# HGRN2's products inside a token tile, cut to 32 keys by their own 32 queries, in four column groups of TensorE

## The chip, the cores and the metric

The kernel runs on one core of one Trainium2 chip. The metric is the device time of one execution in microseconds (us). All times of the profile are counted from the start of the profiled span.

## What is computed

One layer of a decoder: an HGRN2 group of heads (a gated linear recurrence) and an NSA group (sparse attention) side by side, an output projection, and a gated MLP. 512 tokens, 1024 channels. The change touches the HGRN2 group only: 4 heads of width 128, where every key channel of a head has its own decay at each token.

```python
def step(S, inp):                      # per chunk of 64 tokens
    qi, ki, vi, bi = inp               # bi: running sum of the log decays
    o_inter = einsum('bhtk,bhkv->bhtv', qi * exp(bi), S)
    diff = bi[:, :, :, None, :] - bi[:, :, None, :, :]
    dec = where(causal, exp(minimum(diff, 0.0)), 0.0)
    A = einsum('bhtsk,bhsk->bhts', dec * qi[:, :, :, None, :], ki)
    o = o_inter + einsum('bhts,bhsv->bhtv', A, vi)
    ...
```

A holds, for each query token t and each earlier key token s, the product of q and k under the decay between them. The decay depends on the channel, so A is no plain product of two matrices.

## The kernel before

The kernel works on four token tiles of 128 tokens. For HGRN2 it builds, per head and tile, the full 128 × 128 matrix A (tile `hgA`, keys on the partitions, queries in the columns) by halving: first the diagonal (a token with itself), then for L = 1, 2, 4, ..., 64 the products of the keys in an even block of L tokens with the queries in the odd block next to it. At each level the keys carry their decay up to the boundary between the two blocks and the queries theirs from that boundary on, so at each level one plain product serves all blocks of a tile. After each level, keys and queries are multiplied by the decay of a whole block (`tot`), which prepares the next level.

`hg_levels(pr, res)` does this for a pair of heads (`pr` 0 or 1). The second head of a pair (j = 1) has its tokens within a tile in reverse order, so that the blocks that give keys in one head and those of the other interleave, and `early_keys` packs the keys of both heads into one tile `hgE` of full width. One matmul per token tile then makes the products of 128 keys (64 of each head) with 128 queries (64 of each), of which only the blocks next to each other are wanted; a predicated copy on VectorE (L1138, by a mask of constants) picks these out of PSUM (tile `lev`) and puts them into `hgA`. So a level is:

- four matmuls on TensorE (L1129, a block of rows "lev<-hgQ,hgE"), 128 × 128 each, in float32;
- on VectorE (DVE): the keys times their decay (L1130, L1133), the predicated copy (L1138), the queries times theirs (L1141), the next block decay (L1147);
- on ScalarE (ACT): the keys of the next level (L1098, `hgE`).

The diagonal takes four matmuls for each head of the pair (L1109) and a multiplication by the identity for each (L1111).

What surrounds it: the attention of NSA (scores `S`, transposes `F`, values `oT`, at L969 to L1055), the input projections (`pT`, at L141 to L143) and the compression branch (`cps`, L884) run interleaved with the levels. The order is written out by hand: each of these is a Python generator, and a string `ORDER` of letters says which one takes its next step; "l" is `hg_levels(0)` and "m" is `hg_levels(1)`. Each engine then works through its instructions in exactly that order, with semaphores between engines. `G` takes a tile from a ring of 32 buffers of SBUF, `PS` one from the eight PSUM banks.

Some products of the kernel already use part of the columns of TensorE, with the output in the matching partitions of PSUM, so that several such products stand side by side: `values` (L1055, 64 stationary columns, the two heads of a couple in partitions 0 to 63 and 64 to 127), `cmp_hidden` (L884, 64 columns) and `ada_row` (L1293, 32 columns, four groups).

After the levels, `hgA` is the stationary operand of the output products `hgo` (L1224), together with the state between the tiles (L1227).

Of the kernel before, what the change touches and what calls it, by code (L numbers as in the profile page):

```python
# [13 lines left out]
U8 = mybir.dt.uint8  # L14
AF = mybir.ActivationFunctionType
ALU = mybir.AluOpType
# [3 lines left out]
P = 128  # L20
T = 512
NT = T // P
# [37 lines left out]
LEVELS = (1, 2, 4, 8, 16, 32, 64)  # L60
# [3 lines left out]
C_LMASK = 136  # L64
C_CMASK = C_LMASK + sum(P // n for n in LEVELS)
# [10 lines left out]
def shape_constants():  # L76
    c = np.zeros((P, C_COLS), np.float32)
    p = np.arange(P)
    c[:, C_IDENT:C_IDENT + P] = np.eye(P, dtype=np.float32)
    m = [np.broadcast_to(((t[:, None] // (2 * L) == np.arange(64 // L)[None])  # L80
                          & ((t[:, None] // L) % 2 == 0))[:, None], (P, NT, 64 // L)).reshape(P, -1)
         for L in LEVELS for t in (p, P - 1 - p)]
    c[:, C_LMASK:C_CMASK] = np.ascontiguousarray(np.concatenate(m, axis=1).astype(np.uint8)).view(np.float32)
    n = np.arange(32)
# [12 lines left out]
def hybrid_layer_kernel(ctx: ExitStack, tc: tile.TileContext, d: dict, out: bass.AP, dbg=None):  # L97
# [21 lines left out]
    def PS(s="ps"):  # L119
        return psum.tile([P, 512], F32, tag="b", name=nm(s))  # L120
# [142 lines left out]
    mask = cb[:, C_LMASK:C_CMASK].bitcast(U8)  # L263
# [837 lines left out]

    def hg_levels(pr, res):
        TT, KS, QP = HG[pr]
        AD = G([2, NT, P], s="hgA")
        for j in range(2):
            ps = PS("lev")
            for i in range(NT):
                sl = slice(i * P, (i + 1) * P)
                pe.matmul(ps[:, sl], KS[:, j, sl], QP[:, j, sl], start=True, stop=True)  # L1109
            yield  # L1110
            ve.tensor_tensor(AD[:, j], ps.rearrange("p (i t) -> p i t", i=NT),  # L1111
                             ident[:, ::1 - 2 * j].unsqueeze(1).to_broadcast([P, NT, P]), ALU.mult)
# [7 lines left out]
        while L < P:  # L1120
# [3 lines left out]
            m0 = sum(512 // n for n in LEVELS if n < L)  # L1124
            ps = PS("lev")
            pv = ps.rearrange("p (j i n l) -> p j i n l", j=2, i=NT, l=L)
            qt = QP.rearrange("p j (i n two l) -> p j i n two l", i=NT, two=2, l=L)
            for i in range(NT):
                pe.matmul(pv[:, :, i], E[:, i * P:(i + 1) * P], qt[:, :, i, :, 1], start=True, stop=True)  # L1129
# [5 lines left out]
            if 2 * L < P and EPOS == 0:  # L1135
                E = early_keys(KS, 2 * L)
            yield
            ve.copy_predicated(AD.rearrange("p j i (n two l) -> p (j i n) two l", two=2, l=L)[:, :, 1],  # L1138
                               mask[:, m0:m0 + 512 // L].unsqueeze(2).to_broadcast([P, 512 // L, L]),
                               ps.rearrange("p (n l) -> p n l", l=L))  # L1140
# [540 lines left out]
```

## Time and profile before

| | |
|---|---|
| device time, median of 3 runs | 702.78 us (702.70 to 703.16) |
| span of the profiled execution | 701.6 us (the runs' times include about 1.2 us around it) |
| granted TensorE clock | 1.000 |
| busy: PE / PEld / DVE / ACT / POOL | 99% / 82% / 66% / 46% / 16% of the span |
| level products, L1129 | 112 records from 140.8 to 253.0 us |
| diagonal products, L1109 | 32 records from 124.9 to 173.8 us |
| predicated copies, L1138 | 14, 893 ns on average, 12.5 us |

PE is the matmul side of TensorE and PEld its weight loads, POOL is GpSimd, SP issues DMAs. Matmul records overlap in the profile, so a duration of one record is longer than what it adds; what one adds is read from the distance between starts, or from the pieces of the chain of work that ended last. The note "x8" behind a name is the count of records.

### The profile page before, as it was taken

How to read it: one execution, taken by the hardware profiler on the slowest of the kernel's cores; microseconds unless marked ns; L12 is line 12 of the kernel's file. 1: busy time of each engine (PE TensorE's matmuls, PEld its weight loads, DVE VectorE, ACT ScalarE, POOL GpSimd, SP SyncE). 2: the span in 40 equal slices, each digit the busy share in tenths (PEclk: the TensorE clock that was granted, in tenths of full speed). 3: DMA queues.
4: the chain of work that ended last, by engine and by line, in shares of the span. 5: the costliest groups of instructions: out<-in, count | busy, mean ns of one | idle time of the engine just before them, and what ended most of it. 6: DMA issues, size and time to landing. Idle time of an engine off the chain costs nothing.

```text
span 701.6 us, 10075 instructions
## 1 busy us (share of the span) xinstructions
PE 692.7 (99%) x3863; PEld 576.1 (82%) x3864; DVE 461.0 (66%) x882; ACT 324.8 (46%) x618; POOL 108.8 (16%) x101
## 2 busy tenths in 40 slices
PE   8999999999999999999999999999999999999997
PEld 4668898788888889888988888888888888888886
DVE  5588989987889879688756556665555554224224
ACT  5554446565676778345543353444443443111210
POOL 2005021200000000100037527611010110000000
PEclk9999999999999999999999999999999999999999
DMA  9996452558212125243053545424424233134301
GB/s 286 293 290 195 123 160 88 193 192 270 76 47 93 62 77 204 79 143 82 21 166 106 150 126 145 143 69 120 113 67 121 77 103 121 60 94 177 119 32 60
DMA packets 100485, 90.18 MB, mean 129 GB/s; under 512 B 5788, under 2 KB 83412, under 8 KB 100438
## 3 DMA queue, kind: packets, MB, share of 16 engines
q1 hardware_dynamic: 100181, 89.44, 41.6%
q8 instruction: 30, 0.49, 0.3%
q14 instruction: 18, 0.14, 0.1%
q10 hardware_dynamic: 256, 0.11, 0.1%
HBM read 87.43 MB, written 2.11 MB: 128 GB/s over the span
## 4 chain that ended last, share of the span: by engine, by line
PE 81%; DVE 11%; DMA 3%; SPq 2%; ACT 1%; issue 1%; POOL 0%; ACTq 0%; DVEq 0%; POOLq 0%
PE u L142 11%; PE u L143 11%; PE u L141 11%; PE dn L143 6%; PE dn L142 6%; PE dn L141 6%; PE oT L1055 3%; PE F L1027 3%; PE pT L141 2%; PE pT L143 2%; PE pT L142 2%; PE lev L1129 2%; PE oh L141 2%; PE oh L143 2%; PE oh L142 2%; PE S L969 1%
## 5 line engine op out<-in xcount | busy, mean ns | idle before, releaser
L138 DVE TENSOR_TENSOR wlo<-raw,whi 128x1024 fp32r<-128x1024 f32 (+1 forms) x87 | 111.4, 1280 | 130.4 <-ACT whi L137 129.9
L141 PE MATMUL u<-h2h,whi 128*128 128x512 f32 (+1 forms) x360 | 136.7, 380 | 0.0
L142 PE MATMUL u<-h2l,whi 128*128 128x512 f32 (+1 forms) x360 | 136.7, 380 | 0.0
L143 PE MATMUL u<-h2h,wlo 128*128 128x512 f32 (+1 forms) x360 | 136.7, 380 | 0.0
L137 ACT CAST whi<-raw 128x1024 fp32r<-128x1024 f32 (+1 forms) x87 | 89.8, 1032 | 99.6 <-PE dn L143 80.1
L141 PEld LDWEIGHTS u<-h2h,whi 128*128 128x128 f32 x360 | 67.7, 188 | 12.9
L143 PEld LDWEIGHTS u<-h2h,wlo 128*128 128x128 f32 x360 | 67.7, 188 | 12.7
L142 PEld LDWEIGHTS u<-h2l,whi 128*128 128x128 f32 x360 | 67.7, 188 | 12.7
L142 PE MATMUL dn<-wlo,gT 128*128 128x512 f32 (+1 forms) x160 | 62.1, 388 | 0.0
L143 PE MATMUL dn<-whi,gT 128*128 128x512 f32 (+1 forms) x160 | 62.1, 388 | 0.0
L141 PE MATMUL dn<-whi,gT 128*128 128x512 f32 (+1 forms) x160 | 62.0, 388 | 0.0
L1568 POOL TENSOR_TENSOR y<-y,y 128x512 f32<-128x512 f32 x22 | 28.4, 1290 | 165.7 <-DVE y L1563 165.7
L353 POOL TENSOR_TENSOR hrs<-hrs,mhalf 128x4 f32<-128x4 f32 (+2 forms) x16 | 18.3, 1153 | 203.5 <-DVE hrs L352 203.5
L137 ACT CAST gT<-y 128x512 fp32r<-128x512 f32 x20 | 12.4, 621 | 71.7 <-POOL y L1568 71.7
L138 DVE TENSOR_TENSOR gT<-y,gT 128x512 fp32r<-128x512 f32 x20 | 15.0, 750 | 43.0 <-ACT gT L137 43.0
L141 PE MATMUL pT<-hT,whi 128*128 128x512 f32 x96 | 39.2, 408 | 0.0
L143 PE MATMUL pT<-hT,wlo 128*128 128x512 f32 x96 | 37.6, 392 | 0.0
L142 PE MATMUL pT<-hT,whi 128*128 128x512 f32 x96 | 37.5, 391 | 0.0
L1566 ACT ACTIVATE y<-y 128x512 f32<-128x512 f32 x22 | 13.9, 632 | 49.7 <-DVE y L1563 49.7
L142 PEld LDWEIGHTS dn<-wlo,gT 128*128 128x128 f32 x160 | 30.0, 188 | 6.5 <-DVE wlo L138 0.2
L141 PEld LDWEIGHTS dn<-whi,gT 128*128 128x128 f32 x160 | 30.0, 188 | 6.2
L143 PEld LDWEIGHTS dn<-whi,gT 128*128 128x128 f32 x160 | 30.0, 188 | 6.1
(371 smaller groups left out, 1443.6 us busy)
## 6 DMA issues: line engine op xcount, KB each, us to landing
raw<-in_w_up SPq DMA_DIRECT2D x44, 512.0 KB, 4.1
aw<-in_w_ada SPq DMA_DIRECT2D x24, 512.0 KB, 3.9
raw<-in_w_down SPq DMA_DIRECT2D x10, 1024.0 KB, 5.0
ada<-in_w_ada SPq DMA_DIRECT2D x32, 256.0 KB, 6.0
raw<-in_w_in SPq DMA_DIRECT2D x7, 1024.0 KB, 6.2
x<-in_x SPq DMA_DIRECT2D x8, 512.0 KB, 4.6
raw<-in_w_cmp SPq DMA_DIRECT2D x8, 512.0 KB, 4.6
raw<-in_w_out SPq DMA_DIRECT2D x4, 1024.0 KB, 5.9
```

Source lines behind the costliest of these rows:

```text
L137: sc.copy(hi, src)
L138: (eng or ve).tensor_tensor(lo, src, f32(hi), ALU.subtract)
L141: pe.matmul(o, ah, bh, start=start, stop=False, skip_group_check=True)
L142: pe.matmul(o, ah, bl, start=False, stop=False, skip_group_check=True)
L143: pe.matmul(o, al, bh, start=False, stop=stop, skip_group_check=True)
L353: gp.tensor_tensor(o, o, mhalf[:, 0:n], ALU.pow)
L969: pe.matmul(o, QS[i][:, h], KK[g, 0][:, 0:i + 1, bsl], start=True, stop=False)
L1027: pe.transpose(ps[:, j * P:(j + 1) * P], src[:, j * P:(j + 1) * P], ident)
L1055: pe.matmul(oTs[i][r:r + 64, h // 2], VV[:, j, b, g], src[:, q * P:(q + 1) * P], start=(h == 0 and b == 0 and j == 0), stop=False, skip_gr ...
L1129: pe.matmul(pv[:, :, i], E[:, i * P:(i + 1) * P], qt[:, :, i, :, 1], start=True, stop=True)
L1566: sc.activation(y, y, AF.Silu)
L1568: gp.tensor_tensor(ys[0], ys[0], y, ALU.mult)
```

## The change

The 128 × 128 matrix A of a tile is seen as 4 × 4 blocks of 32 tokens. The diagonal and levels 1 to 16 only concern the four blocks on its diagonal: 32 keys with their own 32 tokens. `small_products` makes just these: 16 matmuls a level (four tiles, four groups g) with 32 stationary columns, partitions 32g to 32g + 31 of PSUM as output, and 32 moving columns (16 queries of each head), or, for the diagonal, 32 matmuls of 32 × 32 at one time for both heads. The results gather in one block of 32 columns of `hgA` (`own`, columns 32 to 63 of each tile), by a multiplication with a small diagonal mask and by predicated copies of 128 elements in place of 512. After level 16, `spread` on GpSimd copies the blocks from there to their places and clears the rest; a clear of all of `hgA` (GpSimd too) stands at the start. Levels 32 and 64 (`large_products`) make 16 matmuls of 32 × 32 and 8 of 64 × 64; their results are all wanted, and `large_out` copies them by turns with ScalarE and VectorE. The masks of the constants shrink, and `ORDER` stays as it is.

```diff
-LEVELS = (1, 2, 4, 8, 16, 32, 64)
+LEVELS = (1, 2, 4, 8, 16)
...
+    def columns(ap, off, *dims):
+        return bass.AP(ap.tensor, ap.offset + off, [tuple(ap.ap[0]), *dims])
+
+    def small_products(ps, K, QP, L):
+        for i in range(NT):
+            for g in range(4):
+                o, k = ps[32 * g:32 * g + 32], slice(i * P + 32 * g, i * P + 32 * g + 32)
+                if L:
+                    pe.matmul(columns(o, 16 * i, (64, 2), (L, 16 // L), (1, L)), K[:, k],
+                              columns(QP, i * P + 32 * g + L, (T + 32 * (3 - 2 * g), 2), (2 * L, 16 // L), (1, L)),
+                              start=True, stop=True, skip_group_check=True)
+                else:
+                    for j in range(2):
+                        q = i * P + 32 * (3 - g if j else g)
+                        pe.matmul(o[:, j * P + 32 * i:j * P + 32 * i + 32], K[:, j, k], QP[:, j, q:q + 32], start=True,
+                                  stop=True, skip_group_check=True)
+
+    def large_products(ps, E, QP, L):
+        for i in range(NT):
+            for g in range(P // L):
+                j, n = g % 2, g // 2
+                if j:
+                    n = 64 // L - 1 - n
+                q = i * P + 2 * L * n + L
+                pe.matmul(ps[L * g:L * g + L, i * L:i * L + L], E[:, i * P + L * g:i * P + L * g + L],
+                          QP[:, j, q:q + L], start=True, stop=True, skip_group_check=True)
+
+    def large_out(ps, AD, L):
+        for g in range(P // L):
+            j, n = g % 2, g // 2
+            if j:
+                n = 64 // L - 1 - n
+            (ve.tensor_copy if g % 2 else sc.copy)(AD[L * g:L * g + L, j, :, 2 * L * n + L:2 * L * n + 2 * L],
+                                                   ps[L * g:L * g + L, 0:NT * L].rearrange("p (i t) -> p i t", i=NT))
+
+    def spread(AD):
+        for j in range(2):
+            for g in range(4):
+                w = 3 - g if j else g
+                if w != 1:
+                    gp.tensor_copy(AD[32 * g:32 * g + 32, j, :, 32 * w:32 * w + 32],
+                                   AD[32 * g:32 * g + 32, j, :, 32:64])
+            gp.memset(AD[64 - 64 * j:P - 64 * j, j, :, 32:64], 0.0)
+
     def hg_levels(pr, res):
         TT, KS, QP = HG[pr]
         AD = G([2, NT, P], s="hgA")
-        for j in range(2):
-            ps = PS("lev")
-            for i in range(NT):
-                sl = slice(i * P, (i + 1) * P)
-                pe.matmul(ps[:, sl], KS[:, j, sl], QP[:, j, sl], start=True, stop=True)
-            yield
-            ve.tensor_tensor(AD[:, j], ps.rearrange("p (i t) -> p i t", i=NT),
-                             ident[:, ::1 - 2 * j].unsqueeze(1).to_broadcast([P, NT, P]), ALU.mult)
+        gp.memset(AD, 0.0)
+        own = AD[:, :, :, 32:64]
+        ps = PS("lev")
+        small_products(ps, KS, QP, 0)
+        yield
+        ve.tensor_tensor(own, ps[:, 0:256].rearrange("p (j i t) -> p j i t", j=2, i=NT),
+                         diag32.unsqueeze(2).to_broadcast([P, 2, NT, 32]), ALU.mult)
+        yield
         ve.tensor_tensor(QP, QP, TT, ALU.mult)
...
-            for i in range(NT):
-                pe.matmul(pv[:, :, i], E[:, i * P:(i + 1) * P], qt[:, :, i, :, 1], start=True, stop=True)
+            (small_products if L < 32 else large_products)(ps, E, QP, L)
...
-            ve.copy_predicated(AD.rearrange("p j i (n two l) -> p (j i n) two l", two=2, l=L)[:, :, 1],
-                               mask[:, m0:m0 + 512 // L].unsqueeze(2).to_broadcast([P, 512 // L, L]),
-                               ps.rearrange("p (n l) -> p n l", l=L))
+            if L < 32:
+                m0 = sum(P // n for n in LEVELS if n < L)
+                ve.copy_predicated(own.rearrange("p j i (n two l) -> p (j i) n two l", two=2, l=L)[:, :, :, 1],
+                                   mask[:, m0:m0 + P // L].rearrange("p (a n) -> p a n", a=2 * NT).unsqueeze(3)
+                                   .to_broadcast([P, 2 * NT, 16 // L, L]),
+                                   ps[:, 0:P].rearrange("p (a n l) -> p a n l", a=2 * NT, l=L))
+            else:
+                large_out(ps, AD, L)
+            if L == 16:
+                spread(AD)
```

How this moves instructions, at three places. First TensorE at the diagonal of the first pair (a name is output<-moving operand, stationary operand; a shape is that of the output, and "x3" counts further equal calls). Before:

```order
L1109 MATMUL lev_1488<-hgQ_1237,hgK_730 128x128 [waits DVE_49,Activation_49]
L1109 MATMUL lev_1488<-hgQ_1237,hgK_730 128x128 x3
L834 MATMUL ps_1493<-cb,dst_1372 128x128 [waits DVE_49,Activation_49]
...
L863 MATMUL ps_1528<-cb,wpe_698 128x32 [waits DMAHW5_49,DVE_49,Activation_49]
L1109 MATMUL lev_1545<-hgQ_1237,hgK_730 128x128 [waits Activation_49]
L1109 MATMUL lev_1545<-hgQ_1237,hgK_730 128x128 x3
L141 MATMUL pT_1550<-hT_289,whi_1444 128x512 [waits PE_49,Activation_49]
```

And with the change, at the same place:

```order
L1122 MATMUL lev_1489<-hgQ_1237,hgK_730 32x32 [waits DVE_49,Activation_49]
L1122 MATMUL lev_1489<-hgQ_1237,hgK_730 32x32 x31
L838 MATMUL ps_1522<-cb,dst_1372 128x128 [waits DVE_49,Activation_49]
...
L867 MATMUL ps_1557<-cb,wpe_698 128x32 [waits DMAHW5_49,DVE_49,Activation_49]
L144 MATMUL pT_1574<-hT_289,whi_1444 128x512 [waits Activation_49]
```

The second head's diagonal moves up to the first's place, and its own place is empty. Next, VectorE and ScalarE at level 32 of the first pair; before, VectorE:

```order
L1138 COPY_PREDICATED hgA_1487<-cb,lev_2484 128x16x32
L1141 TENSOR_TENSOR hgQ_1237<-hgQ_1237,hgtot_2392 128x16x32
L1010 RECIPROCAL su_2478<-su_2478 128x2 [waits Activation_49]
L1011 TENSOR_TENSOR su_2478<-su_2478,gates 128x2 [waits DVE_49]
L974 ISA pt_2585,mx_2584<-S_2581,cmask 128x384 [waits PE_49]
```

With the change, VectorE:

```order
L1141 COPY hgA_1487<-lev_2622 32x4x32 [waits Activation_49]
L1141 COPY hgA_1487<-lev_2622 32x4x32 [waits Activation_49,Pool_49]
L1196 TENSOR_TENSOR hgQ_1237<-hgQ_1237,hgtot_2518 128x16x32
L1014 RECIPROCAL su_2616<-su_2616 128x2
L1015 TENSOR_TENSOR su_2616<-su_2616,gates 128x2 [waits DVE_49]
```

and ScalarE, where before only the two `hgE` copies stood:

```order
L1102 COPY hgE_2705<-hgK_1435 128x2x32x8 [waits DVE_49]
L1141 COPY hgA_1487<-lev_2622 32x4x32 [waits Pool_49]
L1141 COPY hgA_1487<-lev_2622 32x4x32 [waits DVE_49]
L1102 COPY hgE_2712<-hgK_730 128x2x4x64 [waits Activation_49]
L1038 COPY pT_2718<-F_2714 128x384 [waits PE_49]
```

One predicated copy on VectorE has become four copies by turns on two engines, each of which waits for the one before. Last GpSimd, which did nothing between the compression branch (`flat`) and the output norm (`hrs`); with the change, from the second pair's clear on:

```order
L875 TENSOR_TENSOR flat_1566<-kv_87_697,pet 128x8x31 x2
L1157 MEMSET hgA_2063 128x1024 [waits PE_49,Activation_49]
L1150 COPY hgA_1487<-hgA_1487 32x4x32 [waits DVE_49,Pool_49]
L1150 COPY hgA_1487<-hgA_1487 32x4x32 [waits Pool_49]
L1150 COPY hgA_1487<-hgA_1487 32x4x32
L1152 MEMSET hgA_1487 64x4x32 [waits Pool_49]
L1150 COPY hgA_1487<-hgA_1487 32x4x32 x2
L1150 COPY hgA_1487<-hgA_1487 32x4x32 [waits Pool_49]
L1152 MEMSET hgA_1487 64x4x32 [waits Pool_49]
```

GpSimd has gained a clear and eight small operations for each pair, behind `flat` and ahead of `hrs`; the first pair's clear stands ahead of `flat`.

More of the change, by code (lines that the diff above doesn't have):

```diff
@@ L64 @@
 C_LMASK = 136
-C_CMASK = C_LMASK + sum(P // n for n in LEVELS)
+C_D32 = C_LMASK + sum(32 // n for n in LEVELS)
+C_CMASK = C_D32 + 64
 C_CAUS = C_CMASK + NT * 32
@@ L79, in shape_constants @@
     c[:, C_IDENT:C_IDENT + P] = np.eye(P, dtype=np.float32)
[L80 to L83, printed above, removed]
+    t = (p % 32, 31 - p % 32)
+    m = [np.broadcast_to(((u[:, None] // (2 * L) == np.arange(16 // L)[None])
+                          & ((u[:, None] // L) % 2 == 0))[:, None], (P, NT, 16 // L)).reshape(P, -1)
+         for L in LEVELS for u in t]
+    c[:, C_LMASK:C_D32] = np.ascontiguousarray(np.concatenate(m, axis=1).astype(np.uint8)).view(np.float32)
+    c[:, C_D32:C_CMASK] = np.concatenate([u[:, None] == np.arange(32)[None] for u in t], axis=1)
     n = np.arange(32)
@@ L262, in hybrid_layer_kernel @@
     ident = cb[:, C_IDENT:C_IDENT + P]
-    mask = cb[:, C_LMASK:C_CMASK].bitcast(U8)
+    mask = cb[:, C_LMASK:C_D32].bitcast(U8)
+    diag32 = cb[:, C_D32:C_CMASK].rearrange("p (j t) -> p j t", j=2)
     vrow = cst.tile([72, P], F32, name="vrow")
@@ L1123, in hg_levels @@
             tv = tot[:, :, 0:2 * nb].rearrange("p j (n two) -> p j n two", two=2)
-            m0 = sum(512 // n for n in LEVELS if n < L)
             ps = PS("lev")
-            pv = ps.rearrange("p (j i n l) -> p j i n l", j=2, i=NT, l=L)
-            qt = QP.rearrange("p j (i n two l) -> p j i n two l", i=NT, two=2, l=L)
-            for i in range(NT):
-                pe.matmul(pv[:, :, i], E[:, i * P:(i + 1) * P], qt[:, :, i, :, 1], start=True, stop=True)
+            (small_products if L < 32 else large_products)(ps, E, QP, L)
             ve.tensor_tensor(kv[:, 0, :, 0], kv[:, 0, :, 0],
```

## The prediction

> **What bounds the kernel now.** I read the page first (which engine, which chain), then busy time by stage, then what the weight loads of TensorE waited for, then the chain piece by piece around the HGRN2 levels.
>
> ```profile
> PE 692.7 (99%) x3863; PEld 576.1 (82%) x3864; DVE 461.0 (66%) x882; ACT 324.8 (46%) x618; POOL 108.8 (16%) x101
> PE 81%; DVE 11%; DMA 3%; SPq 2%; ACT 1%; issue 1%; POOL 0%; ACTq 0%; DVEq 0%; POOLq 0%
> 100.00:140.00 40.00, 39.87 (x237) 32.32 (x235) 36.15 (x93) 23.61 (x76) 7.06 (x10) 1.00 0.42 137
> 140.00:280.00 140.00, 140.00 (x1126) 121.74 (x1123) 121.35 (x296) 95.99 (x228) 0.00 (x0) 1.00 0.39 127
> ```
>
> The first two lines are the page's busy times and its chain by engine; the other two are stretches of the span, with busy time of PE, PEld, DVE, ACT and POOL in that order, then the granted clock, DMA share and GB/s. PE is busy throughout, but its records overlap, so busy alone proves little. What does is that between 138 and 282 us PE hardly waits for another engine:
>
> ```profile
> PEld oT L1055 <- issue: 2.2, 10, 0.4
> PEld S L969 <- issue: 1.4, 8, 0.2
> PEld pT L141 <- ACT pT L1034: 0.4, 1, 0.4
> PEld F L1027 <- ACT pt L1016: 0.3, 1, 0.3
> PEld S L969 <- DVE hgA L1138: 0.2, 1, 0.2
> ```
>
> (us in total, times, longest.) About 1 us of 144 is a wait for ACT or DVE. So from 138 us on, a microsecond of PE time taken out of the stream is a microsecond of the span, as long as DVE (121 of 140 us busy) and ACT (96 of 140) don't take over. All fourteen level blocks lie there. Ahead of 138 us the chain runs on DVE, and the first pair's diagonal lies on it:
>
> ```profile
> 129.58 3.65 DVE flat L871 x4
> 133.23 0.60 DVE hgA L1111
> 133.83 1.13 DVE wlo L138
> 134.96 0.60 DVE hgA L1111
> 135.56 1.13 DVE hgQ L1113
> 137.87 0.30 ACT pt L1016
> 138.21 0.33 PE F L1027
> ```
>
> (Pieces of the chain: start, us, what.) PE waits only 0.3 us there (the row F from ACT pt above), so PE's own path is that close behind.
>
> **The price of a column-grouped product.** The kernel already has such products: oT (stationary 64 columns, two groups, 128 moving), cps (64 columns, two groups, 256 moving) and rows (32 columns, four groups, 256 moving).
>
> ```profile
> 158.95 0.89 PE lev L1129 x8
> 159.84 1.88 PE cps L884 x16
> 161.72 0.87 PE oT L1055 x16
> 162.60 0.43 PE S L969
> 163.02 0.23 PE S L970
> 204.61 0.91 PE lev L1129 x8
> 205.52 1.46 PE oT L1055 x24
> 206.98 0.37 PE S L969
> 249.50 1.90 PE oT L1055 x32
> ```
>
> ```profile
> L1129 PE MATMUL lev<-hgQ,hgE x112: 270/275/328, 140.8 to 253.0; 128*128 128x128 f32 x112
> L1109 PE MATMUL lev<-hgQ,hgK x32: 275/275/377, 124.9 to 173.8; 128*128 128x128 f32 x32
> 216.20 0.64 PE L1293 MATMUL rows<-aacc,ones 128*32 128x256 f32 x8
> 216.77 1.53 PE L1055 MATMUL oT<-pT,VV 128*64 128x128 f32 x24
> ```
>
> A float32 call leaves two records (56 level calls, 112 records), so a level block of four calls is x8 and takes 0.90 us. For oT, eight more records cost 1.90 − 1.46 = 0.44 us. Eight records are two pairs of calls in two passes, so one pass over both groups takes 0.109 us for 128 moving columns. The rest, 1.46 − 3 × 0.44 = 0.14 us, is the way into the column mode; the oT behind cps, already in that mode, doesn't pay it (0.87 = 8 × 0.109). The way out shows on the next full-width matmul: S L969 takes 0.43 where S L970 takes 0.23, so 0.20 us. Together 0.34 us a block. cps gives (1.88 − 0.14) / 8 = 0.217 us a pass for 256 columns, twice oT's: the time goes with the moving columns, 0.85 ns each. And rows, with **four** groups, takes 216.77 − 216.20 = 0.57 us, (0.57 − 0.14) / 2 = 0.215 us a pass: four groups run at once, for the price of one.
>
> A new block of levels 1 to 32 has 16 calls of 32 keys with 32 moving columns: four rounds of four groups, two passes, each 32 × 0.85 = 27 ns, so 0.22 us of streaming. What no row shows is a stream that dense. Its 64 instructions must also be supplied. The nearest rows are two waits of the sequencer, which runs ahead of the engine:
>
> ```profile
> L834 PEldq EVENT_SEMAPHORE  x1: 51/51/51, 113.1 to 113.1; - x1
> L969 PEldq EVENT_SEMAPHORE  x1: 51/51/51, 113.4 to 113.4; - x1
> ```
>
> Between them stand the four L834 and twelve pT matmuls and their loads, 32 instructions in 0.3 us, so some 10 ns each. Were nothing queued ahead, 64 would take 0.64 us. But the second wait at 113.4 belongs to a product behind twelve matmuls of 0.23 us, so the queue holds tens of instructions when a block begins. I take 0.30 us between the ends 0.22 and 0.64, nearer the lower for that reason, and a block at 0.34 + 0.30 = 0.64 us.
>
> **The sum, part by part.**
> - Levels 1 to 32, both pairs: 12 blocks × (0.90 − 0.64) = −3.1 us. Ends: −4.1 (0.56 a block) and +1.0 (0.98 a block).
> - Two of these blocks (158.95, 204.61) are directly followed by cps and oT, which pay for the column mode today; a way in and a way out fall away, some 0.2 us each: −0.4.
> - Level 64: eight calls of 64 × 64, four rounds, two passes of 54 ns, 0.43 + 0.34 = 0.77; 2 × (0.77 − 0.90) = −0.3.
> - Diagonal of the second pair: two blocks of 0.89 become one of 32 calls, 128 instructions. Streaming is 0.44, supply alone 1.28; the middle 0.86, since fewer of so many can stand ready, + 0.34 = 1.20 against 1.78: −0.6.
> - Diagonal of the first pair: on the chain, two DVE operations of 0.60 become one of half their elements together, some 0.35: −0.85. PE's path beside it loses the same 0.6 and had 0.3 to spare, so it allows that.
> - Weight loads of 32 columns: counted with the passes above, as in rows. Nothing more.
>
> So far −5.2 us. DVE, ACT and POOL:
>
> ```profile
> L1138 DVE COPY_PREDICATED hgA<-cb,lev 128x512 f32<-128x512 uint8 x14 | 12.5, 893 | 0.0
> L1169 DVE COPY hgS<-lev 128x128 f32<-128x128 f32 x4 | 1.1, 284 | 0.0
> L1147 DVE TENSOR_TENSOR hgtot<-hgtot 128x256 f32<-128x256 f32 x2 | 0.8, 416 | 0.0
> L1034 ACT COPY pT<-F 128x256 f32<-128x256 f32 x12 | 4.4, 370 | 1.9 <-PE F L1027 1.9
> L1346 POOL MEMSET aw<- 128x512 f32 x2 | 1.1, 526 | 0.0
> L871 POOL TENSOR_TENSOR flat<-kv,pet 128x248 f32<-128x248 f32 x4 | 4.2, 1065 | 15.1 <-DVE pet L864 15.1
> L871 DVE TENSOR_TENSOR flat<-kv,pet 128x248 f32<-128x248 f32 x4 | 3.7, 971 | 0.1
> ```
>
> - DVE: ten predicated copies shrink from 512 to 128 elements (893 to some 284 ns each), four become two copies of 128 or one of 256. Some 9 us less work in all; I count it as zero beyond the first diagonal, since PE is the bound.
> - ACT: per pair two copies of 128 and one of 256 elements, at most 0.37 us each, 2.2 us in all, inside 44 us that ACT is free.
> - POOL: per pair a clear of 1024 elements (two of 526 ns) and eight small operations, each at most as long as a flat operation: under 8.5 us. POOL does nothing from 140 to 280 us. The first clear is queued ahead of flat, and behind operations that end by 114.4 us, so it is done long before DVE's 133.2. The spread begins after level 16 and must end before level 32 goes out: 17 us for the first pair and 9 for the second (by the predicated copies of these levels today).
> - While POOL's flat runs, DVE's flat of 248 elements takes 971 ns, and an equally large operation (416 ns row, 256 elements) less than half. So spread can stretch DVE by up to some 4 us a pair; the 9 us saved cover it.
> - At level 32 the four copies alternate ACT, DVE, ACT, DVE, each waiting for the one before, because they write one tile. Behind the waiting DVE copy stands the query product hgQ for level 64, behind the waiting ACT copy the keys of level 64. Four times 0.3 us plus hand-overs is 1.4 us in the place of 0.7. The first pair's level 64 comes 4 us later, so nothing; the second pair's comes at once:
>
> ```profile
> 251.30 0.67 DVE L1141 TENSOR_TENSOR hgQ<-hgQ,hgtot 128x512 f32<-128x512 f32 x1
> 252.22 1.06 PE L1129 MATMUL lev<-hgQ,hgE 128*128 128x128 f32 x8
> ```
>
> hgQ ends at 251.97 and PE begins at 252.2. The 0.7 us, less the room of 0.2 and what DVE gains just ahead, leaves PE waiting: +0.3, ends 0 and +1.
>
> The profiled span is 701.6 us; the runs' median 702.78 includes 1.2 us around it, which doesn't change. Sum −5.2 + 0.3 = −4.9: 702.8 − 4.9 = 697.9 us (span 696.7).
>
> **Rivals.**
> A, slower: four groups don't overlap at this size, each small matmul takes its own 27 ns. A block is 32 × 0.027 + 0.34 = 1.21 us, +0.31 × 12 = +3.7; level 64 is the same, +0.6; the second diagonal 64 × 0.027 + 0.34 = 2.08, +0.3; the first about 0, as PE becomes its bound; −0.4 for the shared switches, +0.3 at level 64. Sum +4.5, 707.3 us. It decides from (0.90 − 0.34) / 32 = 17.5 ns a matmul on. Against it: rows shows four groups at once. For it: nothing in the trace runs denser than oT's 0.44 / 8 = 55 ns a matmul, and if that were the floor, the time would be near 720.
> The Trainium skill speaks against the change here: TensorEngine Tiling (Array Packing), Performance Considerations, Instruction Overhead, says that a matmul of one moving column lasts as long as one of about 60 cycles, and not to take the tiling factor from a dimension that is already small. At the 2.4 GHz of TensorE: Matmul & The Clock Gate this is 25 ns, which if paid per matmul one after the other is rival A, by an estimate some 0.5 us better; if paid by groups at once it leaves my sum alone. No run here shows which yet.
>
> B, no change: PE's gain is taken back by the new hand-overs, since PE's next level needs what stands behind them, or by bank order (one lev tile fewer per pair shifts which PSUM bank each later tile takes, and with it some waits of S and F). It decides if these cost 5 us; but for the place above, the trace has 4 us of room at each, which speaks against it. 702.8 us.
>
> C, nearly nothing: supply is at its upper end (0.98 a block): 12 × 0.08 = +1.0, second diagonal 1.28 + 0.34 = 1.62 (−0.2), the rest as above (−0.4, −0.3, −0.85, +0.3): −0.5, 702.3 us. Supply halfway to that gives 700.
>
> **How the numbers follow.** Forecast 0.64, its own range 695.6 (level blocks at their lower end, −1.0, the second diagonal too, −0.4, no wait at level 64, −0.3, and half a microsecond of PE's other waits gone) to 700.5. C and what lies between it and the forecast 0.13, half of it faster. B 0.05. A 0.15, the 720 end 0.03. Of 702.8, 0.2% (1.4 us) is about what a measurement of this kernel can tell from none. Faster 0.64 + 0.06 = 0.70; same 0.07 + 0.05 = 0.12; slower 0.18. Up to 705 the range takes in C, B and the milder part of A, and leaves some 0.17 out.
>
> **What would show it.** Right: lev blocks of x32 with some 0.45 us in the chain, the matmul behind a lone block 0.2 us longer than now, hgA copies near 0.3 us, PE still without waits for DVE from 138 us on. Wrong: lev blocks of 0.9 us and more (A or C), PE waiting for ACT hgA or DVE hgQ at levels 32 and 64, POOL copies over 1 us, or the shift from PE lost to a wait at the output projection.

## The result, and the profile after

The changed kernel takes 698.84 us (median of 4 runs, 698.66 to 699.39) against 702.75 for the kernel before on the same chip: ratio 0.9943, 95% interval 0.9929 to 0.9957. Run again beside later experiments it took 699.29 against 702.89, 0.9947 [0.9935, 0.9960]. The forecast was 697.9.

From the page: busy times and the chain by engine; then, from the busy times by stretch, 140 to 280 us (PE, PEld, DVE, ACT, POOL, then clock, DMA share, GB/s).

```profile
PE 687.0 (98%) x4263; PEld 566.5 (81%) x4264; DVE 453.2 (65%) x882; ACT 326.0 (47%) x624; POOL 117.5 (17%) x119
PE 77%; DVE 10%; ACT 5%; DMA 4%; SPq 2%; issue 1%; POOL 0%; ACTq 0%; DVEq 0%
```

```profile
140.00:280.00 140.00, 138.13 (x1490) 115.60 (x1478) 116.33 (x300) 97.92 (x233) 8.67 (x18) 1.00 0.41 133
```

400 more matmul records, and yet TensorE is busy for less: 138.13 of 140 us where it was 140.00. The chain has less PE (77% for 81%) and more ACT (5% for 1%) and DMA (4% for 3%). What PE's weight loads wait for between 130 and 280 us (us in total, times, longest; the lines that are new or longer than before) shows where:

```profile
PEld lev L1133 <- ACT hgE L1102: 1.1, 2, 0.9
PEld cps L888 <- DMA raw<-in_w_cmp: 0.9, 1, 0.9
PEld ps L1253 <- ACT hvT L1244: 0.7, 1, 0.7
PEld F L1031 <- ACT pt L1020: 0.6, 2, 0.4
```

Three waits of 0.7 to 0.9 us stand where there was hardly one. The first line names ScalarE's `hgE`, but at the second level 64 VectorE's `hgQ` is what comes last (see e4_copies_last). The product blocks themselves, on the timeline of PE (start, us, line, output<-moving, stationary; records):

```profile
124.91 0.86 PE L1122 MATMUL lev<-hgQ,hgK 128*32 128x32 f32 x64
139.80 0.47 PE L1116 MATMUL lev<-hgQ,hgE 128*32 128x32 f32 x32
206.25 0.46 PE L1133 MATMUL lev<-hgQ,hgE 128*32 128x32 f32 x32
207.26 0.65 PE L1253 MATMUL ps<-cb,hvT 128*128 128x128 f32 x4 [0.56 <-ACT hvT L1244]
```

A level block of 32 records is through in 0.46 us, a diagonal of 64 in 0.86. The helpers on the other engines, by the tile `hgA` (durations in ns, min/median/max):

```profile
L1188 DVE COPY_PREDICATED hgA<-cb,lev x10: 291/299/447, 143.8 to 237.7; 128x128 f32<-128x128 uint8 x10
L1141 ACT COPY hgA<-lev x6: 237/256/367, 214.8 to 255.1; 32x128 f32<-32x128 f32 x4, 64x256 f32<-64x256 f32 x2
L1150 POOL COPY hgA<-hgA x12: 279/292/1342, 199.0 to 241.4; 32x128 f32<-32x128 f32 x12
L1162 DVE TENSOR_TENSOR hgA<-lev,cb x2: 407/412/418, 132.8 to 174.3; 128x256 f32<-128x256 f32 x2
```

**Where the time went.** I took the start of the same TensorE instruction in both traces and followed the difference, after minus before, along the program. Negative is earlier.

| place (us, after) | difference before and behind it | change |
|---|---|---|
| first diagonal, 125 to 139.8 | −0.12, −1.06 | −0.94 |
| eight lone blocks of levels 1 to 32 | −0.19 to −0.37 each | −2.57 |
| two blocks followed by cps or oT (157, 201) | −0.50, −0.52 | −1.02 |
| cps at 163 waits for its weights | −2.33, −1.30 | +1.03 |
| level 8 and the second diagonal, 169 to 171 | −1.30, −2.47 | −1.17 |
| level 32 of the first pair, with the wait for hvT behind it | −3.61, −3.34 | +0.27 |
| level 64 of the first pair | −3.63, −3.75 | −0.12 |
| level 64 of the second pair, with its wait for hgQ and hgE | −4.36, −3.75 | +0.61 |

The rows add up to −3.91. The stream stood at −0.12 ahead of them, and some 0.28 is lost between them, 0.2 of it ahead of `rows` at 213 us; so it stands at −3.75 from 250 us on. The last 0.18 is won at 298 us, behind the changed stage, in a wait for the output norm; the last instruction comes 3.93 us earlier. Valued at the lone blocks' mean of −0.32, levels 8 and 32 that stand with something else give −0.32 each, so the twelve blocks together gave about −4.2 us and the second diagonal −0.85. Gains of 6.3 us in all, of which some 2.4 went into the three waits.

The largest, at cps, ends a chain that starts with another transfer (pieces of the chain: start, us, what):

```profile
136.11 0.37 SPq L207
136.52 9.75 DMA raw<-in_w_in
146.29 1.06 ACT whi L140
147.38 1.23 DVE wlo L141
...
155.38 0.94 ACT whi L140
156.35 1.24 DVE wlo L141
157.60 0.37 SPq L207
158.02 5.00 DMA raw<-in_w_cmp
163.06 1.94 PE cps L888 x14
```

There are two buffers `raw`. The projection weights (w_in) come into one of them at 146.3 us, are split in two steps with softmax work between, and only when the second split is done, at 157.6, can the compression weights (w_cmp) be fetched into it. In the kernel before PE came to this cps at 164.41 and the data had landed at 162.5, 1.9 us ahead. Now PE would be there at 162.1, and the data land at 163.0. So of the 0.9 us of wait 0.4 is PE's gain beyond the old margin, and 0.5 is the transfer's own delay: its chain starts 1.0 us later than before, with a landing of w_in at 146.3 that was at 145.3.

### The profile page after: what moved, and what is told of

Read it like the earlier page. It is cut to its first block, busy times and chain, and to the rows that moved or that the text cites. A ratio compares the mean times of both kernels' runs of the same rounds, so it can differ in the third digit from the quotient of the medians.

```text
span 697.6 us, 10902 instructions
## 1 busy us (share of the span) xinstructions
PE 687.0 (98%) x4263; PEld 566.5 (81%) x4264; DVE 453.2 (65%) x882; ACT 326.0 (47%) x624; POOL 117.5 (17%) x119
## 4 chain that ended last, share of the span: by engine, by line
PE 77%; DVE 10%; ACT 5%; DMA 4%; SPq 2%; issue 1%; POOL 0%; ACTq 0%; DVEq 0%
PE u L146 11%; PE u L144 11%; PE u L145 11%; PE dn L144 6%; PE dn L145 6%; PE dn L146 6%; PE pT L144 2%; PE pT L146 2%; PE pT L145 2%; PE oT L1059 2%; PE F L1031 2%; PE oh L144 2%; PE oh L146 2%; PE oh L145 2%; DMA raw<-in_w_in 1%; DVE rows L399 1%
## 5 line engine op out<-in xcount | busy, mean ns | idle before, releaser
L1616 ACT ACTIVATE y<-u,cv 128x512 f32<-128x512 f32 x44 | 33.9, 772 | 0.0
```

Source lines behind the costliest of these rows:

```text
L1616: sc.activation(y, u, AF.Identity, bias=cv[:, 132 + c:133 + c], scale=cv[:, 88 + c:89 + c])
```

## The experiments

Each ratio is to the kernel before on the same chip. The last column is from the trace: how much later (+) the end of the TensorE stream comes than in the changed kernel. Since the first 60 us move by −0.5 to +1.1 us from one profile to the next, the streams are aligned at 60 us. The changed kernel's own second profile gives −0.24, so smaller differences mean nothing. The runs of one kernel spread by 0.5 to 2.6 us.

| | median us | ratio, 95% interval | end of stream |
|---|---|---|---|
| e1_double | 703.04 | 1.0001 [0.9992, 1.0010] | +3.6 |
| e2_group_order | 701.52 | 0.9978 [0.9969, 0.9987] | +2.15 |
| e11_fourfold | 710.92 | 1.0114 [1.0098, 1.0129] | +11.0 |
| e3_dve_only | 702.51 | 0.9995 [0.9986, 1.0004] | −0.46 against before |
| e7_diag_twice | 699.61 | 0.9950 [0.9936, 0.9963] | +0.7 |
| e8_large_full | 699.70 | 0.9955 [0.9942, 0.9967] | +0.2 |
| e4_copies_last | 698.62 | 0.9941 [0.9929, 0.9954] | −0.34 |
| e5_ada_later | 698.51 | 0.9937 [0.9923, 0.9951] | −0.1 |
| e9_halves | 698.86 | 0.9941 [0.9928, 0.9953] | −0.78 |
| e6_both | 698.45 | 0.9938 [0.9925, 0.9950] | −0.67 |
| e10_halves_copies | 698.73 | 0.9944 [0.9932, 0.9957] | −0.4 |
| e12_after_again | 699.29 | 0.9947 [0.9935, 0.9960] | −0.24 |

**What a block costs: e1_double.**

```diff
             (small_products if L < 32 else large_products)(ps, E, QP, L)
+            if L < 32:
+                small_products(ps, E, QP, L)
```

> Every product block of levels 1 to 16 is issued twice (the same 16 calls, to the same place), ten blocks in all, so the added time is the price of 16 calls without a way into or out of the column mode. Theory (four groups run at once; a lone block measured 0.39 us in the chain): 0.25 to 0.30 us more a block, 2.5 to 3.0 us in the TensorE stream, of which up to 1 us vanishes in the new wait for the compression weights at 164 us: 700.5 to 701.8 us. Rival A (each small matmul takes its own 27 ns): 0.87 more a block, about 707 us. Rival C (supply of instructions at 10 ns each): 0.64 more a block, about 705 us. Rival D (the block is nearly all switch of mode): 0.1 more a block, 699 to 699.8 us.

On the timeline of PE, the first doubled block, and on that of PEld one further on:

```profile
139.74 0.77 PE L1116 MATMUL lev<-hgQ,hgE 128*32 128x32 f32 x64
```

```profile
172.09 0.64 PEld L1116 LDWEIGHTS lev<-hgQ,hgE 128*32 128x32 f32 x63
174.12 0.11 PEld L1116 LDWEIGHTS lev<-hgQ,hgE 128*32 128x32 f32 x1 [1.40 <-issue]
```

0.77 in the place of 0.47: 16 calls, 32 records, add 0.30 us, 9.4 ns a record, and in the stream a block adds about 0.3. That is the theory's price; A (0.87), C (0.64) and D (0.1) fall. The time is still 1.2 us above the expected range. Most of this is in the second fence: in the middle of one block, before its last load, PE stood still for 1.4 us with nothing to wait for. Without this stop the time would be about 701.6, an estimate that takes the stop of this one profile for all ten runs. The wait at cps, too, did not shrink as expected but grew to 1.2 us, for the compression weights landed 1.2 us later than in the changed kernel.

**Do the groups overlap: e2_group_order.** The same 16 calls of levels 1 to 16, all four tiles of a group before the next group.

```diff
-        for i in range(NT):
-            for g in range(4):
+        for n in range(4 * NT):
+            for g in ((n // NT) if L else n % 4,):
+                i = n % NT if L else n // 4
```

> In the blocks of levels 1 to 16 the same 16 calls stand in another order: all four tiles of one column group, then those of the next, so that neighbouring calls share a group. Theory (the low price comes from four different groups running at once): matmuls of one group follow one another, 32 of 27 ns, some 0.87 us a block in the place of 0.25, +0.5 to +0.6 us a block, ten blocks: 703 to 705 us. Rival (a matmul this small costs only its issue, 8 to 10 ns, whatever its neighbour): no change, 698.5 to 699.2 us.

```profile
139.84 0.91 PE L1117 MATMUL lev<-hgQ,hgE 128*32 128x32 f32 x32
```

The block (first level, timeline of PE) takes 0.91 us, 0.44 more, with the same records. In the stream nine of the ten blocks add 0.38 to 0.44, one 0.24. The price is thus 0.30 + 0.44 = 0.74 us for 32 records, 23 ns each, when neighbours share a group, and 9.4 ns when they don't: a factor of 2.5, not 4. The overlap of the groups is what the low price rests on; the rival that a call is cheap whatever stands beside it falls. At 701.5 us the time lies below the 703 to 705 expected: of the 4.1 us only 2.15 reach the end, since PE comes later to its waits. The one at cps gives back 1.05 us, the one for hvT 0.63 and that ahead of `rows` 0.2. Whether matmuls of one group wait for each other or for the weight loads between them isn't separated here.

The Trainium skill, TensorEngine Tiling (Array Packing), Performance Considerations, Instruction Overhead, gives every matmul about 60 cycles however short it is. By the 2.4 GHz of the Trainium skill's TensorE: Matmul & The Clock Gate, What's actually happening, that is 25 ns as an estimate. The 23 ns of this run agree with it as long as neighbours share a column group; for neighbours in different groups the 9.4 ns of e1_double differ from it, and the measurement decides. The 27 ns that the prediction took from the moving columns are hardly further off than 25, so this run doesn't tell an overhead of each call from time by columns.

**Where the supply ends: e11_fourfold.** Each block of levels 1 to 16 four times.

```diff
             (small_products if L < 32 else large_products)(ps, E, QP, L)
+            if L < 32:
+                for _ in range(3):
+                    small_products(ps, E, QP, L)
```

> Every product block of levels 1 to 16 is issued four times. From the doubled block (0.46 us of records became 0.76) each repeat costs 0.30 us: 10 x 3 x 0.30 = 9.0 us more TensorE time, 2 us of it at most taken up by waits that stand there now: 706 to 708 us, if the price of a call stays what it is. Rival (instructions are fetched in pieces of 16 KB, and the 1.4 us that TensorE stood in the middle of one doubled block at 172.6 us, with such a fetch at 171.7 us, is a fetch that came too late): blocks of 256 instructions then meet a fetch each, with stops of 1 us or more in most of them, and the time is above 712 us.

The first block and the first stop, on the timeline of PE, and then waits of PEld from 130 to 280 us:

```profile
140.22 1.31 PE L1116 MATMUL lev<-hgQ,hgE 128*32 128x32 f32 x128
145.33 0.38 PE L888 MATMUL cps<-raw,flat 128*64 128x256 f32 x1 [1.56 <-issue]
```

```profile
PEld S L973 <- issue: 2.9, 10, 1.2
PEld lev L1116 <- issue: 2.7, 8, 1.0
PEld F L1031 <- issue: 0.8, 1, 0.8
```

A block is 1.31 us, 0.28 a repeat, so the price of a call holds. But the time lies between the two ranges. Four stops with no releaser (1.56 at cps, 1.2, 1.0 and 0.8), in or shortly behind a block, are 4.6 us, more than the 2.9 that lie above 708. They come at four of the ten blocks, so neither side had it right: the price holds, and now and then PE stands still. The page counts the pieces in which instructions are fetched, on their own DMA queue, for the changed kernel and for this one:

```profile
q8 instruction: 33, 0.54, 0.3%
```

```profile
q8 instruction: 41, 0.67, 0.4%
```

Each piece is 16 KB; eight more for the 1920 added records of loads and matmuls. The stop in e1_double, 172.7 to 174.1 us, comes 1 us after such a piece started and ends 2.4 us after that start; the four stops of this run end 2.2 to 2.7 us after the start of a piece (at 142.6, 164.3, 175.3 and 210.7 us). Fifteen other pieces of this run between 130 and 280 us pass without such a stop. That PE waited for a piece is inferred from this coincidence; the trace names no releaser. The Trainium skill, Runtime: NRT & Kernel Launch, Instruction fetch mechanics, has it that instructions come in blocks of 16 KiB and that crossing into the next is mostly hidden, since dispatch is slower than the fetch. The pieces agree; with blocks this dense the stops of 0.8 to 1.6 us speak against "mostly hidden". In the changed kernel itself the longest stop of this kind is 0.4 us.

**Is it TensorE or VectorE: e3_dve_only.** The kernel before, with VectorE's work of the changed one.

```diff
-            ve.tensor_tensor(AD[:, j], ps.rearrange(...), ident[:, ::1 - 2 * j]..., ALU.mult)
+            if j:
+                ve.tensor_tensor(AD[:, 1, 0:2], ps[:, 0:256].rearrange(...), ident[:, ::-1]..., ALU.mult)
...
-            ve.copy_predicated(AD.rearrange(...)[:, :, 1], mask[:, m0:m0 + 512 // L]..., ps...)
+            ve.copy_predicated(AD.rearrange(...)[:, 0:P // L, 1], mask[:, m0:m0 + P // L]..., ps[:, 0:P]...)
```

> The kernel before, with its full-width products, but VectorE is given the changed kernel's smaller work: predicated copies of 128 elements and one diagonal multiplication of 256 a pair (the rest of the level results is left out, and the tile is cleared by GpSimd at the start). Theory (from 138 us on TensorE's own work is the bound; only the first diagonal lies on VectorE): -0.85 us at the first diagonal and within 0.4 us of nothing behind it, 701.6 to 702.2 us. Rival (the gain comes from the relief of VectorE): most of the 3.9 us, 698.8 to 700 us.

The stretch 140 to 280 us of this kernel:

```profile
140.00:280.00 140.00, 140.00 (x1126) 121.94 (x1125) 113.67 (x295) 96.42 (x227) 0.95 (x1) 1.00 0.39 128
```

VectorE does 113.67 us of work for 121.35 before, PE is busy throughout as before, and from 139 us to the end the stream stays where it was: −0.46 us, all of it won at the first diagonal. So 7.7 us taken off VectorE behind 140 us are worth nothing there, and the gain of the change behind 139 us comes from TensorE. The −0.85 us expected at the first diagonal was too much, and the time lies above the expected range. At the first diagonal relief of VectorE alone gives half of what the change gives (−0.94); PE, with its diagonal products still whole, then works from 136 to 139 us without a wait.

**The first diagonal: e7_diag_twice.**

```diff
+        ve.tensor_tensor(own, ps[:, 0:256].rearrange(...), diag32..., ALU.mult)
         ve.tensor_tensor(own, ps[:, 0:256].rearrange(...), diag32..., ALU.mult)
```

> The changed kernel with the diagonal multiplication on VectorE (412 ns) issued twice for each pair. Theory (the first pair's lies on the chain through VectorE, the second's beside TensorE's work): the TensorE stream 0.3 to 0.4 us later from 134 us to 160 us, nothing more at the second pair (174 us). At 164 us TensorE waits 0.9 us for the compression weights, which takes the delay up as far as the transfer itself doesn't move: 698.8 to 699.3 us. Rival (TensorE's own stream is the bound already at the first diagonal): no shift at 140 us.

VectorE's timeline at the first diagonal:

```profile
132.51 0.40 DVE L1162 TENSOR_TENSOR hgA<-lev,cb 128x256 f32<-128x256 f32 x1
132.94 0.42 DVE L1164 TENSOR_TENSOR hgA<-lev,cb 128x256 f32<-128x256 f32 x1
```

VectorE's work behind comes 0.4 us later, the TensorE stream 0.25 later at 137 us, and 0.13 is left of it behind cps; at the second diagonal (174 us) nothing is added. So the first diagonal is on the chain and the second isn't, and the wait at cps takes up half. The end is then 0.7 us later, and the time above the expected range: 0.18 came at 195 us in a wait for hvT and 0.35 at the second pair's level 64, where PE waited 1.2 us for 0.9. That this is the doubled multiplication's doing isn't shown.

**Levels 32 and 64 alone: e8_large_full.**

```diff
     def large_products(ps, E, QP, L):
+        if L >= 32:
+            pv = ps.rearrange("p (j i n l) -> p j i n l", j=2, i=NT, l=L)
+            qt = QP.rearrange("p j (i n two l) -> p j i n two l", i=NT, two=2, l=L)
+            for i in range(NT):
+                pe.matmul(pv[:, :, i], E[:, i * P:(i + 1) * P], qt[:, :, i, :, 1], start=True, stop=True)
+            return
...
```

> Levels 32 and 64 with the products of the kernel before (four calls of 128 by 128, of which the wanted blocks are copied as now); levels 1 to 16 and the diagonal as in the changed kernel. Theory (TensorE time counts one to one there): 0.45 to 0.55 us more at each level 32, 0.1 to 0.3 at each level 64, 1.1 to 1.7 us in all, less what an idle wait at the second level 64 takes up (0.5 us of its 0.9 if the copies wait for the longer block too, then nothing): 699.6 to 700.6 us. Rival (these levels are bound by the hand-over of the copies): below 0.4 us in all, 698.8 to 699.2 us.

Level 32 of the first pair, timeline of PE (the copies into hgA read the same blocks from their places in the full product):

```profile
205.46 1.06 PE L1131 MATMUL lev<-hgQ,hgE 128*128 128x128 f32 x8
```

The block is 1.06 us of records for 0.46, but in the trace only 0.2 us arrive at the end. The stream was 0.2 us ahead already behind cps, which the edit doesn't touch, so counted from there it is 0.44. The wait for hvT behind the first level 32 falls from 0.7 to 0.2, the one at the second level 64 from 0.9 to 0.6. By the runs it is 0.4 to 0.9 us slower than the changed kernel, which the intervals don't separate. So here TensorE's time no longer counts one to one: by the table above these four blocks save some 0.9 us of stream (0.32 a level 32, 0.12 a level 64), and about half of it reaches the end. The forecast of 1.1 to 1.7 was too high.

**The wait at the second level 64: e4_copies_last.**

```diff
-            else:
-                large_out(ps, AD, L)
...
             if 2 * L < P and EPOS == 1:
                 E = early_keys(KS, 2 * L)
+            if L >= 32:
+                large_out(ps, AD, L)
```

> At levels 32 and 64 the copies of the results into hgA are issued behind the product of the queries (VectorE) and the copy of the next keys (ScalarE) instead of ahead of them. Theory (the second pair's level 64 waits 0.9 us for hgE and hgQ because these stand behind four copies that alternate between the engines): that wait vanishes or shrinks below 0.2 us, 698.0 to 698.4 us. Rival (the keys would be late anyway, behind the softmax work of ScalarE): the wait stays above 0.6 us, 698.6 to 699.1 us.

ScalarE and VectorE of the changed kernel, then of this one:

```profile
247.19 0.26 ACT L1141 COPY hgA<-lev 32x128 f32<-32x128 f32 x1 [0.83 <-DVE hgA L1141]
247.47 0.62 ACT L1102 COPY hgE<-hgK 128x512 f32<-128x512 f32 x1
247.54 0.30 DVE L1141 COPY hgA<-lev 32x128 f32<-32x128 f32 x1 [0.39 <-ACT hgA L1141]
247.85 0.69 DVE L1196 TENSOR_TENSOR hgQ<-hgQ,hgtot 128x512 f32<-128x512 f32 x1
```

```profile
246.39 0.62 ACT L1102 COPY hgE<-hgK 128x512 f32<-128x512 f32 x1 [0.66 <-DVE hgK L1181]
246.92 0.25 ACT L1141 COPY hgA<-lev 32x128 f32<-32x128 f32 x1
246.28 0.69 DVE L1194 TENSOR_TENSOR hgQ<-hgQ,hgtot 128x512 f32<-128x512 f32 x1
```

In the changed kernel the keys of level 64 stand behind a copy that waits 0.83 us for VectorE's, and the queries behind one that waits 0.39 us for ScalarE's. The queries come last: hgQ ends at 248.54, hgE at 248.09, and PE begins at 248.69. Ahead of the copies the queries are done 1.05 us earlier and the keys 0.56 (aligned; this profile is 0.52 early), and the wait at level 64 falls from 0.9 to 0.2 us. The theory is right on the cause and wrong on the worth: the stream gains 0.74 at level 64, 0.29 of it is lost right behind, where F now waits for the copies into hgA, and 0.34 is left at the end, for softmax pieces (F behind ACT pt, 0.9 us in four waits for 0.6 in two) are late next. In the runs the difference can't be seen.

**The wait at cps: e5_ada_later.** The load of modulation weights behind sum 8 goes out with that behind sum 9.

```diff
-                if c + ADW == D:
+                if c + ADW == D and n != 8:
                     ada_load()
+                    if n == 9:
+                        ada_load()
```

> One load of modulation weights (512 KB, issued at 139.6 us in the changed kernel and not needed before 157.5) is issued behind the next one, after 144 us. Theory (it shares the bandwidth with the projection weights that ScalarE waits for until 146.3 us, and this delay runs on through the split of those weights to the transfer of the compression weights that TensorE awaits at 163 us): the projection weights land 0.8 to 1.3 us earlier, the compression weights 0.6 to 1.3 us earlier, and the wait of 0.9 us at cps is gone or below 0.3 us: 697.9 to 698.3 us. Rival (the chain through the softmax work of ScalarE and VectorE sets the release of the buffer, not the transfer): the projection weights land earlier, but the compression weights within 0.3 us of now, and the time stays at 698.6 to 699.1 us.

SP's issue of the deferred load, two at once, and ScalarE's first split:

```profile
144.93 0.98 SPq L1321 DMA_DIRECT2D aw<-in_w_ada  x2
```

```profile
146.84 1.05 ACT L140 CAST whi<-raw 128x1024 fp32r<-128x1024 f32 x1 [1.44 <-DMA raw<-in_w_in]
```

The theory falls in its first step, and the rival's first half with it. The load moved from 139.6 to 144.9 us, yet ScalarE starts its split at 146.84, which is 146.23 aligned, for 146.29. This load had not delayed the projection weights; cps still waits 0.8 us. The run's median of 698.51 would look like a gain of 0.3 to 0.8 us, and the trace says that nothing changed: a warning of how far medians here can be trusted.

What does delay the landing may be an instruction piece. Between 137 and 147 us the changed kernel has one on that DMA queue, the kernel before none:

```profile
q8 instruction: 1, 0.02, 0.7%
```

0.7% of 16 DMA engines over 10 us is 1.1 us of one of them. The second half of the projection weights comes in on the 16 engines from 144.4 to 146.3 us in the changed kernel, from 144.6 to 145.3 in the kernel before. The landing is told by 16 signals, read here as one for each engine: in the changed kernel fourteen come by 144.7 us, one at 145.2 and the last at 146.3. The same picture stands in e1_double at the compression weights: there a piece starts at 159.8 us, in the middle of the transfer, fifteen signals come by 162.7 and the last at 164.2; in the changed kernel, which has no piece there, all come between 162.6 and 163.0. One late engine by about the time of a piece speaks for it, but no run moved a piece alone, so the cause stays inferred.

**The same wait from the other side: e9_halves.** The projection weights in four transfers.

```diff
-        loads.append(load(f"hv{'eo'[p]}", [KT, 256], *[(..., hv_view[:, :, h, p]) for h in range(2)]))
+        loads.append(load(f"hv{'eo'[p]}", [KT, 256], *[(..., hv_view[:, 4 * a:4 * a + 4, h, p])
+                                                     for a in range(2) for h in range(2)] if not p else ...))
```

> The load of projection weights that ScalarE awaits at 146.3 us (1 MB, in two transfers of all eight row blocks for half of the columns each) is made in four transfers, the first four row blocks ahead of the last four, so that the first split needs only half of it. Theory (the compression weights come late because their buffer is freed by a chain that starts with this landing: split, softmax work, second split at 157.6 us, transfer): the first split starts 1 to 1.5 us earlier (ScalarE is free from 144.8 us), the compression weights land 0.8 to 1.5 us earlier, TensorE's wait of 0.9 us at cps falls below 0.2, and the stream stays 0.6 to 0.9 us earlier to the end: 698.0 to 698.3 us. Rival (the release is set by ScalarE's and VectorE's own order of work or by TensorE): the first split moves, the second by less than 0.3 us, and the time stays within 0.3 us of the changed kernel's.

ScalarE's two splits, and SP's issue of the compression weights (start, us):

```profile
144.48 1.05 ACT L140 CAST whi<-raw 128x1024 fp32r<-128x1024 f32 x1
153.45 1.05 ACT L140 CAST whi<-raw 128x1024 fp32r<-128x1024 f32 x1
```

```profile
155.78 0.92 SPq L210 DMA_DIRECT2D raw<-in_w_cmp  x2
```

Aligned at 60 us (this profile is 0.30 early there), both splits and the issue are 1.5 us earlier than in the changed kernel, cps no longer waits, and the stream is 1.03 us ahead behind it. So the chain from the landing of the projection weights is the cause of this wait: shown. Of the 1.03, 0.25 are lost again at the next waits:

```profile
PEld lev L1136 <- ACT pT L1041: 1.0, 1, 1.0
PEld ps L1256 <- ACT hvT L1247: 0.8, 1, 0.8
```

(waits of PEld, 130 to 280 us) and 0.78 stays to the end. The runs put it at 698.86 against 699.29 for the changed kernel on the same chip, a difference of the expected sign inside the intervals, and above the 698.0 to 698.3 expected.

**Both waits at once: e6_both and e10_halves_copies.** The edits above, put together.

> Both edits together: the copies behind hgQ and hgE, and the load behind the next one. If the two waits are independent the gains add: 697.0 to 697.6 us. If each only moves the stream up to the same next wait (ScalarE's copy of the value projection at 207 us is the candidate), 697.8 to 698.4 us.

> The same load in halves, and the copies of levels 32 and 64 behind hgQ and hgE. The copies alone brought the stream 0.47 us forward at the second level 64, of which 0.34 lasted to the end. If the two waits are independent: 0.9 to 1.2 us off the changed kernel, 697.6 to 698.0 us. If the time won at cps is lost again at the value projection (ScalarE hvT, 207 us, a wait of 0.7 us now): about 0.4 us off, 698.3 to 698.6 us.

Neither adds up. e6_both ends 0.67 us ahead, of which 0.34 was won at cps though e5_ada_later shows that its edit does nothing there; the wait at cps is 0.5 to 0.9 us from one profile to the next. e10_halves_copies is 1.02 us ahead behind cps and about as much at 264 us: the copies win 0.74 at level 64, and F right behind loses 0.63 in its wait for them. Another 0.6 is lost at 312 us, where a small load and the supply of instructions hold up PE in this one profile. In the runs 698.45 and 698.73 lie just above the ranges expected, and are the changed kernel's time within its interval. All of these beat the kernel before by about as much as the change itself does; that one of them beats the change isn't shown by time.

> The changed kernel itself, beside the others on the same chip: 698.6 to 699.2 us.

It came at 699.29, just above the upper edge.

## Why the prediction was right

The sign, the size and the place hold: −3.9 us against −4.9, some 3 of it from TensorE behind 138 us. The sum came out near for two errors that partly cancel: the gains were 6.3 us for 5.2, the losses 2.4 for 0.3. That the total is within 1 us is in part luck.

- **TensorE is the bound from 138 us, so its time counts one to one.** Right at the start, as e3_dve_only shows, and no longer so once 2 to 3 us were gained: PE caught up with a transfer, with ScalarE's hvT and with VectorE's hgQ, and e8_large_full shows about 0.44 us at the end for some 0.9 us of stream.
- **A block at 0.64 us.** Too dear. The lone blocks gain 0.32 on average, so a block is at 0.58; the stream alone was measured as 0.30 (e1_double), just what was taken, so it is the 0.34 for the way in and out that was too high, by some 0.06: what stands behind a lone block takes 0.02 to 0.11 us longer than it did, where 0.2 was expected. All twelve blocks with their shared switches gave about −4.2 for −3.5. The stream, though, isn't 27 ns for a round of four: it is 38 (4 × 9.4), and its agreement with 0.30 came from the allowance for supply.
- **Two blocks ahead of cps and oT.** −0.51 each against −0.32 alone: 0.19 of shared switch, as forecast (0.2).
- **Level 64**: −0.12 at the first pair for −0.13.
- **The diagonals.** The first −0.94 for −0.85, on VectorE's chain with PE's right beside it (e7_diag_twice, e3_dve_only). The second about −0.85 for −0.6: the allowance for 128 instructions in a row was too large.
- **Wait at the second level 64**: the place and the cause, hgQ behind the alternating copies, were right (e4_copies_last), the size was not: +0.61, or about +0.75 without what the block itself saves, for +0.3.
- **What failed**: the sum left nothing for waits at places other than the levels. "The trace has 4 us of room at each" speaks of the new hand-overs; the compression weights, which had 1.9 us, weren't looked at. PE came 2.3 us earlier and the weights 0.5 us later: a wait of 0.9, and 1.03 us lost. Together with the 0.6 at hvT this is rival B's outcome in a mild form, a gain taken back in part, but neither by the new hand-overs nor by bank order: by other work that was just in time.
- **Rival A** falls by e1_double (9.4 ns a matmul for 27) and by e2_group_order, which is what A describes for neighbours of one group; at 25 ns its sum would have been about 0.9 us better, not 0.5. **C** falls by e1_double. C's fear is not groundless: in blocks two and four times as long the stream does stop now and then.
- **Signs.** The blocks of 0.46 us and the hgA copies near 0.3 came as named for a right forecast. Of the signs named for a wrong one two came as well: PE waits for hgQ at the second level 64, and GpSimd copies last over 1 us. The second cost nothing, for they end 4 us and more ahead of level 32's first copy into hgA, which waits for them.
- **Zeros.** GpSimd's spread shows no cost on VectorE where the two meet: a query product partly beside it lasts as long as one without it,

```profile
198.77 0.69 DVE L1196 TENSOR_TENSOR hgQ<-hgQ,hgtot 128x512 f32<-128x512 f32 x1
242.07 0.69 DVE L1196 TENSOR_TENSOR hgQ<-hgQ,hgtot 128x512 f32<-128x512 f32 x1
```

  the first while GpSimd copies (199.0 to 202.9 us), the second with GpSimd idle. A softmax piece of 128x512 (L978) takes 0.68 us at 240.88 beside the copies and 0.69 at 242.87 without them. It is GpSimd's own copy that goes from 0.29 to as much as 1.34 us.

## What to carry to other kernels

Where an engine is the bound over a long stretch, read for every transfer and hand-over there how long ahead of it the data arrive: the smallest of these margins, not the engine's share, says how much of a gain can be kept. Here 1.9 us of margin was used up by the first 2.3 us, and the transfer itself came 0.5 us later. Small matmuls in column groups are cheap if neighbouring calls go to different groups; at this size the order of the loops decides over a factor of 2.5. Below half a microsecond in 700, align two traces at a common instruction and read the shift, since medians of five runs showed a gain of a kernel whose stream had not moved.

## What had not been expected of the hardware

- A matmul of 32 stationary and 32 moving columns (float32, one of two records) takes 9.4 ns between neighbours of other column groups and 23 ns between neighbours of its own.
- PE stopped for 0.8 to 1.6 us without any releaser, in some of the blocks of 128 and 256 dense instructions, none of this size in the changed kernel's blocks of 64.
- The 16 engines of one transfer of 512 KB finished within 0.7 us of each other in the kernel before and within 1.9 in the changed one, where one engine alone was last, and stayed at 1.9 when a competing load of 512 KB was moved out of its way (e5_ada_later).
